# Expert weights in buffers of 2 MB, gate and up stored together, in a two-layer diffusion block

## The chip, the cores and the metric

The kernel runs on one core of a Trainium2 chip. The time is that of one execution on the device, in microseconds (us), from launch to the last result; lower is better. A core has TensorE (PE in the profile, with its weight loads as PEld), VectorE (DVE), ScalarE (ACT), GpSimd (POOL) and SyncE (SP), which here issues nearly all transfers. Sixteen DMA engines move data between DRAM and SBUF, the on-chip memory of 128 partitions.

## The reference, cut to what matters

A block of two layers works on 512 latent and 256 context tokens of width 1024. Each layer is a mixer (attention with retention in the first layer, RWKV with window attention in the second) and then 16 expert feed-forwards; an expert takes the 64 latent tokens that fit it best, in the first layer also 32 context tokens.

```python
def expert_choice_ffn(h, w_router, w_gate, w_up, w_down):
    cap = EC_FACTOR * N // N_EXPERTS                       # 64 latent, 32 context
    aff = softmax(h @ w_router)
    gate, idx = top_k(swapaxes(aff, 1, 2), cap)
    xs = h[idx]
    u = silu(xs @ w_gate) * (xs @ w_up)                    # per expert, 1024 x 1536 each
    y = (u @ w_down) * gate                                # per expert, 1536 x 1024
    return zeros.at[idx].add(y)

for layer in range(2):
    x_lat, x_ctx = mixers of the layer
    x_lat += g2 * expert_choice_ffn(h_lat, w[layer])
    if layer == 0:
        x_ctx += cg2 * expert_choice_ffn(h_ctx, w[layer])
return rmsnorm(x_lat, final_g)
```

All is float32. The three matrices of one expert hold 18.9 MB, those of the 16 experts of a layer 302 MB.

## The kernel before

`build` runs `mixer0`, `moe(0)`, `mixer1` and `moe(1)`. The change is in the two expert stages, `moe`.

An expert's 1536 hidden columns are worked in three chunks c of 512. `weights(c)` (L1909) takes four buffers from `wslot` (L1828) and loads the chunk: for i = 0 the gate rows k = 0 to 3 and the up rows k = 0 to 3, for i = 1 those of k = 4 to 7. A buffer is 128 partitions by 2048 float32: 1 MB, 8 KB in each partition, and `lay_out` (L2127) stores the weights in DRAM so that a partition's 8 KB are one contiguous row. `hidden` (L1919) multiplies the 64 latent tokens with gate and up, at each k first gate, then up (L1924, tile `gu`); `hidden_ctx` (L1933) does the same for 32 context tokens (L1937, tile `guc`). In the first layer the order of chunks is gu 0, guc 0, guc 1, gu 1, gu 2, guc 2. `turn` transposes the result. Then `down` (L1987) works three chunks of the down matrix, each in two buffers of 1 MB, for latent (L1992, `ydn`) and context tokens (L1996, `ydc`); in the last expert of the first layer all context chunks come first. The last down chunk of the kernel is loaded as four pieces of 512 KB.

The buffers are rings, used in turn. In the first layer the ring has 7 buffers (`open_ring(7)`, L730), in the second 12 (L1634) and 4 more of the pool `ring2` (L1824). A load into a buffer waits until TensorE has read what the buffer held. All these loads are issued in order by SP (L1915 and L2024). TensorE's order is written out by hand (`manual_schedule`), that of the other engines is the planner's.

`after` (L1822, L1873, L1960) names pairs of buffers that must not load too early. Into each buffer of such a pair POOL copies a few values of a late result (L1834), so that its load waits for that result: the logits of the router, the first selected tokens, the first context selection. In the second layer these are the pairs 6 and 7, the first four down buffers.

At the end of the second layer `fin` (L2063) takes three buffers of the ring again: the final gain in the first, four output tiles in the other two. When the first layer's stage closes, `mixer1` places its own tiles where the ring was, among them `lv` (loaded at L846).

Of the kernel before, what the change touches and what calls it, by code (L numbers as in the profile page):

```python
# [11 lines left out]
F32 = mybir.dt.float32  # L12
# [8 lines left out]
D = 1024  # L21
# [3 lines left out]
E, FF = 16, 1536  # L25
# [74 lines left out]
class Kern:  # L100
# [203 lines left out]
    def mixer0(self):  # L304
        nc, io, tc = self.nc, self.io, self.tc
# [41 lines left out]
        for t in range(6):  # L347
# [6 lines left out]
            for k0 in range(0, 8, 4):  # L354
# [4 lines left out]
                for i in range(4):  # L359
                    dst, src = aT[k0 + i][:, 128 * t:128 * t + 128], pt[:, 128 * i:128 * i + 128]  # L360
# [11 lines left out]
        for k in range(8):  # L372
            for (a, b, v) in ((0, 256, 1), (256, 768, 0)):
                x = aT[k][:, a:b]
# [352 lines left out]
        self.in_st = ExitStack()  # L727
        self.inp = self.in_st.enter_context(tc.tile_pool(name="in1", bufs=2))
        tc.swap_default_side()
        self.open_ring(7)  # L730

    def out_weights(self, l, w):

# [57 lines left out]
    def mixer1(self):  # L791
        nc, io, tc = self.nc, self.io, self.tc
# [771 lines left out]
        while min(nj.values()) < 6 or fins or min(nfin) < 2 or win:  # L1564
# [7 lines left out]
            for sl in slots:  # L1572
                if sl.gen is None and sets:
                    ok = [k for k in units if np_[k] < min(6, nj[k] + 2)
                          and all((tile_of[k[0]][np_[k]], 2 * k[1] + i) in fed for i in range(2))]
                    if ok:
                        k = min(ok, key=lambda k: np_[k])
# [32 lines left out]
            if wo is not None and min(nj.values()) < 6:  # L1610
                if not proj:
                    ready = [t for t in (3, 4, 2, 5) if nfin[t - 2] == 2 and lack[t]] + [
                        t for t in (3, 4, 2, 5) if 4 in lack[t]]
                    if ready:
                        t = ready[0]
# [15 lines left out]
            self.x[t] = self.xp.tile([128, D], F32, name=f"x{t}")  # L1631
            nc.sync.dma_start(self.x[t], xd[t - 2])
        tc.swap_default_side()
        self.open_ring(12)  # L1634
        st_f.close()
        self.route_open(1)
        routes = []
# [53 lines left out]
    def moe(self, l, out=None):  # L1691
        nc, io, tc = self.nc, self.io, self.tc
# [4 lines left out]
        ctx_on = l == 0  # L1697
# [102 lines left out]
        def split(g, pieces=1):  # L1800

            g.yh = mw.tile([128, D], F32R, name="yh", bufs=1)
            g.yl = mw.tile([128, D], F32R, name="yl", bufs=1)
            n = D // pieces
            for i in range(pieces):
                s = slice(n * i, n * i + n)
                nc.scalar.activation(g.yh[:, s], g.y[:, s], AF.Copy, scale=g.gate[:, 0:1])
                nc.vector.scalar_tensor_tensor(g.yl[:, s], g.y[:, s], g.gate[:, 0:1], g.yh[:, s].bitcast(F32),
                                               OP.mult, OP.subtract)

        def scatter(g):
            for t in range(g.n):
                for h in range(2):
                    pb = self.bank("scp")
                    s, w = slice(512 * h, 512 * h + 512), g.back[:, 128 * t:128 * t + 128]
                    nc.tensor.matmul(pb, w, g.yh[:, s], start=True, stop=False)
                    nc.tensor.matmul(pb, w, g.yl[:, s], start=False, stop=True)  # L1817
                    xs = self.x[g.a + t][:, s]
                    nc.vector.tensor_tensor(xs, pb, xs, OP.add)  # L1819
                yield None  # L1820

        taken, after = [0], {1: self.lgt[0:64, 1, 0:1]} if ctx_on else {}  # L1822

        more = 0 if ctx_on else 4  # L1824
        if more:
            wp = st.enter_context(tc.tile_pool(name="ring2", bufs=more))

        def wslot(nm):  # L1828
            pool = wp if taken[0] % (self.slots + more) >= self.slots else self.ring
            t = pool.tile([128, 2048], F32, name=nm, tag="ring")  # L1830

            w = after.get(taken[0] // 2)
            if w is not None:
                nc.gpsimd.tensor_copy(t[0:64, 0:1], w)  # L1834
            taken[0] += 1
            return t
# [5 lines left out]
        def at(e, place, gen, result=None):  # L1842
            shade.setdefault((e, place), []).append((gen, result))

        def run(e, place):
            for gen, result in shade.pop((e, place), ()):
                r = next(gen, None)
                if result is not None:
                    result[0][result[1]] = r
# [28 lines left out]
        for e in range(E):  # L1878
# [17 lines left out]
            def turn(c, sg, sc):  # L1896
                pt = self.bank("utp")
                for b in range(4):
                    nc.tensor.transpose(pt[:, 64 * b:64 * b + 64], sg[:, 128 * b:128 * b + 128], self.ident[0:64, 0:64])  # L1899
                nc.scalar.activation(uT[:, 4 * c:4 * c + 4], pt[:, 0:256].rearrange("p (b s) -> p b s", b=4), AF.Copy)  # L1900
                if ctx_on:
                    pt = self.bank("utc")
                    for b in range(2):
                        nc.tensor.transpose(pt[:, 64 * b:64 * b + 64], sc[:, 128 * b:128 * b + 128],  # L1904
                                            self.ident[0:64, 0:64])
                    nc.vector.tensor_copy(uTc[:, 4 * c:4 * c + 4].rearrange("p (h b) s -> p b h s", h=2),  # L1906
                                          pt[:, 0:128].rearrange("p (b h s) -> p b h s", b=2, h=2))

            def weights(c):  # L1909

                ws = [], []
                for i in range(2):
                    for w, wt in zip(("moe_w_gate", "moe_w_up"), ws):
                        t = wslot("we")
                        nc.sync.dma_start(t, io[w][l, e, c, i])  # L1915
                        wt += [t[:, 512 * k:512 * k + 512] for k in range(4)]
                return ws

            def hidden(ws):  # L1919
# [26 lines left out]
            if ctx_on and e == 0:  # L1946
# [4 lines left out]
                ws = weights(0)  # L1951
# [4 lines left out]
                ws = weights(1)  # L1956
# [7 lines left out]
            for c in range(3):  # L1964
# [5 lines left out]
                else:  # L1970
                    ws = weights(c)
# [15 lines left out]
            def down(c, wt, lat):  # L1987
                for i in range(4):
                    f = 4 * c + i
                    if lat:  # L1990
                        for h in range(2):
                            nc.tensor.matmul(y[64 * h:64 * h + 64, :], uT[:, f], wt[i][:, 512 * h:512 * h + 512],  # L1992
                                             start=f == 0, stop=f == 11, tile_position=(0, 64 * h))
                    else:
                        for j in range(4):
                            nc.tensor.matmul(yc[32 * j:32 * j + 32, 0:256], uTc[:, f], wt[i][:, 256 * j:256 * j + 256],  # L1996
                                             start=f == 0, stop=f == 11, tile_position=(0, 32 * j))
# [18 lines left out]
                        return gen  # L2016
            wts = []
            for c in range(3):
                wt = []
                for i in range(2):  # L2020
                    t, src = [v.rearrange("p (f n) -> p f n", f=2) for v in (wslot("wd"), io["moe_w_down"][l, e, c, i])]

                    for n in ((0, 2),) if (l, e, c) != (1, E - 1, 2) else ((0, 1), (1, 2)):
                        nc.sync.dma_start(t[:, n[0]:n[1]], src[:, n[0]:n[1]])  # L2024
                    wt += [t[:, 0], t[:, 1]]
                wts.append(wt)
                if ctx_on and e + 1 == E:

                    if c == 0:
                        turn(*prev)  # L2030
                    down(c, wt, False)
                    continue
                for lat in ((False, True), (True, False))[c % 2] if ctx_on else (True,):
                    down(c, wt, lat)
                if c == 0:
                    turn(*prev)
                run(e, 3 + c)
# [11 lines left out]
            if a == 1:  # L2049
                def late(g=g, e=e):  # L2050
                    split(g, 1 if e + 1 < E else 2)
                    if e + 1 < E:
                        yield
                    yield from scatter(g)
                gen = late()
                if e + 1 < E:
                    for p in (0, 1, 2, 3, 3):
                        at(e + 1, p, gen)
                elif out is None:
                    self.tail = gen  # L2060
                else:

                    fin, norms = [self.ring.tile([128, 2048], F32, name="fin", tag="ring") for _ in range(3)], []  # L2063
                    nc.gpsimd.dma_start(fin[0][:, 0:D], io["final_g"].rearrange("(o n) -> o n", o=1).to_broadcast([128, D]))
                    for t, _ in enumerate(gen):
                        for n in norms:
                            next(n, None)
                        norms.append(self.final(out, t, fin))
                        next(norms[-1])
                    for n in norms:  # L2070
                        drain(n)
# [10 lines left out]
    def final(self, out, t, buf):  # L2082

        nc = self.nc
        x, o, fg = self.x[2 + t], buf[1 + t // 2][:, D * (t % 2):D * (t % 2) + D], buf[0][:, 0:D]
        rs = self.norm_tile(x, o, apply=False)
        yield
        nc.vector.scalar_tensor_tensor(o, x, rs, fg, OP.mult, OP.mult)
        nc.sync.dma_start(out[0, 128 * t:128 * t + 128], o)
# [36 lines left out]

def lay_out(arrays):  # L2127

    for n in ("moe_w_gate", "moe_w_up"):
        w = arrays[n].reshape(2, E, 2, 4, 128, 3, 512)  # L2130
        arrays[n] = np.ascontiguousarray(w.transpose(0, 1, 5, 2, 4, 3, 6)).reshape(2, E, 3, 2, 128, 2048)
    w = arrays["moe_w_down"].reshape(2, E, 3, 2, 2, 128, D)
    arrays["moe_w_down"] = np.ascontiguousarray(w.transpose(0, 1, 2, 3, 5, 4, 6)).reshape(2, E, 3, 2, 128, 2048)


# [17 lines left out]
```

## Time and profile before

| | us |
|---|---|
| median of 3 runs | 3020.55 |
| lowest, highest of them | 3016.89, 3022.68 |
| the profiled execution | 3012.17 |
| its span, first to last instruction | 3010.4 |
| expert stage of layer 0, steady experts | 640 to 1420 |
| expert stage of layer 1, after its first expert | 2323 to 2990 |

The profiled execution lies 8.4 us below the median. "Issue" in the profile is time in which an engine waited for nothing that the profile shows. A wait is put down to what came last before the engine went on. Matmuls are pipelined, so a busy PE is not a PE at its peak, and a stretch in which PE waits a little before every matmul can look nearly full.

### The profile page before, as it was taken

The numbers are of one execution on the slowest core, as the hardware profiler recorded it, in microseconds if no ns is written. First come the engines' busy times: TensorE is split into PE (matmuls) and PEld (weight loads), VectorE is DVE, ScalarE is ACT, GpSimd is POOL, SyncE is SP. The second block draws the span as 40 slices with busy tenths as digits, with TensorE's granted clock in tenths as the row PEclk, the third lists the DMA queues.
The fourth block names the chain that finished last, engine by engine and source line by source line (L and its number), as shares of the span: only waits on it lengthen the run. The fifth ranks groups of instructions, "written<-read, shape, count | busy, mean of one in ns | idle before, by whom it ended". The sixth has DMA issues, their size and how long they took to land.

```text
span 3010.4 us, 48424 instructions
## 1 busy us (share of the span) xinstructions
PE 2708.7 (90%) x19606; PEld 1547.0 (51%) x19606; DVE 1324.3 (44%) x3546; ACT 741.4 (25%) x1718; POOL 472.4 (16%) x597
## 2 busy tenths in 40 slices
PE   7999999799999999999878888799987988888987
PEld 4787776544444444444466666587653332333322
DVE  4323664534234234322375777677654332223312
ACT  3212443211111111100263544266321111000111
POOL 2332002200000000000174553411210000000000
PEclk9999999799999999999987988899888999999999
DMA  9764001488988988888642334311349999999997
GB/s 328 249 242 163 26 12 64 156 355 337 362 343 339 362 333 349 361 332 362 245 124 80 92 95 125 107 36 31 117 181 375 420 420 420 420 420 420 420 420 319
DMA packets 217919, 779.52 MB, mean 259 GB/s; under 512 B 28919, under 2 KB 115360, under 8 KB 138080
## 3 DMA queue, kind: packets, MB, share of 16 engines
q1 hardware_dynamic: 210528, 752.33, 64.4%
q0 software_dynamic: 3872, 12.52, 1.2%
q10 hardware_dynamic: 3296, 11.58, 1.0%
q8 instruction: 155, 2.54, 0.3%
q14 instruction: 68, 0.56, 0.1%
HBM read 745.68 MB, written 30.67 MB: 258 GB/s over the span
## 4 chain that ended last, share of the span: by engine, by line
PE 57%; DMA 26%; DVE 9%; ACT 3%; POOL 2%; issue 2%; SPq 0%; POOLq 0%; ACTq 0%; DVEq 0%
DMA we<-in_moe_w_up_dram 18%; PE gu L1924 12%; DMA wd<-in_moe_w_down_dram 7%; PE ydn L1992 6%; PE guc L1937 4%; PE pj L926 3%; PE ydc L1996 3%; PE pj L411 2%; PE op L774 2%; PE pj L412 2%; PE pj L413 2%; PE op L1556 2%; PE adap L231 1%; PE sc L593 1%; PE pe L1398 1%
## 5 line engine op out<-in xcount | busy, mean ns | idle before, releaser
L1924 PE MATMUL gu<-we,xs 128*64 128x512 f32 x3072 | 721.3, 599 | 79.0 <-DMA we<-in_moe_w_up_dram 75.1
L1924 PEld LDWEIGHTS gu<-we,xs 128*64 128x64 f32 x3072 | 226.8, 137 | 537.7 <-issue 392.5
L1992 PE MATMUL ydn<-wd,uT 128*64 128x512 f32 x1536 | 352.9, 600 | 3.0 <-DMA wd<-in_moe_w_down_dram 2.1
L1930 DVE TENSOR_TENSOR sg<-gu,sg 64x512 f32<-64x512 f32 x96 | 66.5, 693 | 482.1 <-ACT sg L1929 481.5
L1929 ACT ACTIVATE sg<-gu 64x512 f32<-64x512 f32 x96 | 56.7, 591 | 872.1 <-PE gu L1924 872.1
L1776 POOL DMA_INDIRECT xg<-xnd,idx x22 | 20.9, 949 | 1276.0 <-DVE gate L1781 913.6
L1992 PEld LDWEIGHTS ydn<-wd,uT 128*64 128x64 f32 x1536 | 101.4, 137 | 200.6 <-issue 178.9
L1937 PE MATMUL guc<-we,xs 128*32 128x256 f32 x3072 | 183.7, 384 | 19.1 <-DMA we<-in_moe_w_up_dram 19.1
L926 PE MATMUL pj<-aL,wblk 128*128 128x512 f32 x504 | 159.8, 452 | 0.0
L1937 PEld LDWEIGHTS guc<-we,xs 128*32 128x32 f32 x3072 | 98.6, 111 | 96.6 <-DMA we<-in_moe_w_up_dram 26.3
L411 PE MATMUL pj<-ah,wblk 128*128 128x384 f32 (+1 forms) x320 | 109.5, 343 | 1.1 <-ACT ah L380 1.0
L926 PEld LDWEIGHTS pj<-aL,wblk 128*128 128x128 f32 x504 | 100.0, 212 | 18.6
L412 PE MATMUL pj<-al,wblk 128*128 128x384 f32 (+1 forms) x320 | 107.7, 337 | 0.3 <-DVE al L382 0.3
L413 PE MATMUL pj<-ah,wblk 128*128 128x384 f32 (+1 forms) x320 | 107.4, 336 | 0.0
L1819 DVE TENSOR_TENSOR x<-scp,x 128x512 f32<-128x512 f32 x144 | 92.4, 684 | 30.9 <-PE scp L1817 29.8
L1996 PE MATMUL ydc<-wd,uTc 128*32 128x256 f32 x1536 | 91.6, 383 | 2.1 <-DMA wd<-in_moe_w_down_dram 2.1
L1906 DVE COPY uTc<-utc 128x128 f32<-128x128 f32 x48 | 14.0, 292 | 177.1 <-PE utc L1904 176.7
L2047 DVE TENSOR_TENSOR yp<-ydn,gbc 64x512 f32<-64x512 f32 x64 | 44.1, 689 | 103.0 <-PE ydn L1992 100.0
L1796 DVE TENSOR_SCALAR xs<-xst,gm,modT 128x128 f32<-128x128 f32 (+1 forms) x88 | 34.9, 398 | 102.8 <-PE xst L1788 99.6
L1942 DVE TENSOR_TENSOR sc<-guc,sc 64x256 f32<-64x256 f32 x48 | 20.4, 425 | 126.7 <-ACT sc L1941 126.6
L1900 ACT ACTIVATE uT<-utp 128x256 f32<-128x256 f32 x96 | 36.0, 375 | 150.6 <-PE utp L1899 149.7
L1382 DVE STREAM_TRANSPOSE Zbd<-X 64x256 f16<-64x256 f16 x144 | 62.8, 436 | 23.4 <-ACT X L1376 21.0
(421 smaller groups left out, 4667.9 us busy)
## 6 DMA issues: line engine op xcount, KB each, us to landing
we<-in_moe_w_gate_dram SPq DMA_DIRECT2D x192, 1024.0 KB, 19.8
we<-in_moe_w_up_dram SPq DMA_DIRECT2D x192, 1024.0 KB, 9.9
wd<-in_moe_w_down_dram SPq DMA_DIRECT2D x190, 1024.0 KB, 10.7
adaw<-in_ada_w_dram SPq DMA_DIRECT2D x48, 1024.0 KB, 6.6
wraw<-in_od_w_in_dram SPq DMA_DIRECT2D x33, 512.0 KB, 4.3
wraw<-in_ev_w_in_dram SPq DMA_DIRECT2D x19, 512.0 KB, 6.9
fb<-B SPq DMA_DIRECT2D x24, 256.0 KB, 2.4
BK<-fb SPq DMA_DIRECT2D x24, 256.0 KB, 3.1
```

Of the source, the lines that this page charges most:

```text
L411: nc.tensor.matmul(pb[:m, :384], w[:, 0, k, 0:m], ah[k][:, t], start=k == 0, stop=False)
L412: nc.tensor.matmul(pb[:m, :384], w[:, 0, k, 0:m], al[k][:, t], start=False, stop=False)
L413: nc.tensor.matmul(pb[:m, :384], w[:, 1, k, 0:m], ah[k][:, t], start=False, stop=k == 7)
L774: nc.tensor.matmul(o, a[:, i, k], cut[h, k][:, j], start=k + i + j == 0, stop=k == 7 and i == 1)
L926: nc.tensor.matmul(pb[:, :n], w[:, i, k], a[j][:, k], start=k + i + j == 0, stop=k == 7 and i == 1)
L1382: nc.vector.transpose(Zd[h], X[hd[h]])
L1819: nc.vector.tensor_tensor(xs, pb, xs, OP.add)
L1924: nc.tensor.matmul(gu[64 * j:64 * j + 64, :], g.xs[:, k, 64 * a:64 * a + 64], ws[j][k], start=k == 0, stop=k == 7, tile_position=(0, 64 * j))
L1930: nc.vector.tensor_tensor(sg, gu[64:128], sg, OP.mult)
L1937: nc.tensor.matmul(guc[32 * j:32 * j + 32, 0:256], q.xs[:, k, 32 * a4:32 * a4 + 32], ws[j // 2][k][:, 256 * (j % 2):256 * (j % 2) + 256], ...
L1992: nc.tensor.matmul(y[64 * h:64 * h + 64, :], uT[:, f], wt[i][:, 512 * h:512 * h + 512], start=f == 0, stop=f == 11, tile_position=(0, 64 * h))
L1996: nc.tensor.matmul(yc[32 * j:32 * j + 32, 0:256], uTc[:, f], wt[i][:, 256 * j:256 * j + 256], start=f == 0, stop=f == 11, tile_position=(0 ...
```

## The change

Gate and up of a chunk half are stored as one tensor `moe_w_gate_up`, so that a partition's row holds the four gate rows and behind them the four up rows: 16 KB contiguous in DRAM, 2 MB in one load. A down chunk becomes one load of 2 MB with rows of 16 KB too. An expert's 18 loads become 9. The first layer's ring has 4 buffers of 2 MB (64 KB in each partition, 56 KB before), the second layer's 6 and 2 more (128 KB in all, as before). The keys of `after` count buffers and not pairs, and so name the same bytes. The last down chunk is still loaded in four pieces of 512 KB. `fin` takes two buffers of 2 MB.

```diff
@@ end of mixer0 @@
-        self.open_ring(7)
+        self.open_ring(4)
@@ end of mixer1 @@
-        self.open_ring(12)
+        self.open_ring(6)
@@ moe @@
-        more = 0 if ctx_on else 4
+        more = 0 if ctx_on else 2
...
-            t = pool.tile([128, 2048], F32, name=nm, tag="ring")
+            t = pool.tile([128, 4096], F32, name=nm, tag="ring")
-            w = after.get(taken[0] // 2)
+            w = after.get(taken[0])
...
                 for i in range(2):
-                    for w, wt in zip(("moe_w_gate", "moe_w_up"), ws):
-                        t = wslot("we")
-                        nc.sync.dma_start(t, io[w][l, e, c, i])
-                        wt += [t[:, 512 * k:512 * k + 512] for k in range(4)]
+                    t = wslot("we")
+                    nc.sync.dma_start(t, io["moe_w_gate_up"][l, e, c, i])
+                    for j in range(2):
+                        ws[j].extend(t[:, 2048 * j + 512 * k:2048 * j + 512 * k + 512] for k in range(4))
...
-                for i in range(2):
-                    t, src = [v.rearrange("p (f n) -> p f n", f=2) for v in (wslot("wd"), io["moe_w_down"][l, e, c, i])]
-                    for n in ((0, 2),) if (l, e, c) != (1, E - 1, 2) else ((0, 1), (1, 2)):
-                        nc.sync.dma_start(t[:, n[0]:n[1]], src[:, n[0]:n[1]])
-                    wt += [t[:, 0], t[:, 1]]
+                t, src = [v.rearrange("p (f n) -> p f n", f=4) for v in (wslot("wd"), io["moe_w_down"][l, e, c])]
+                step = 4 if (l, e, c) != (1, E - 1, 2) else 1
+                for n in range(0, 4, step):
+                    nc.sync.dma_start(t[:, n:n + step], src[:, n:n + step])
+                wt = [t[:, f] for f in range(4)]
...
-                    fin, norms = [self.ring.tile([128, 2048], F32, name="fin", tag="ring") for _ in range(3)], []
+                    fin, norms = [self.ring.tile([128, 4096], F32, name="fin", tag="ring") for _ in range(2)], []
@@ final @@
-        x, o, fg = self.x[2 + t], buf[1 + t // 2][:, D * (t % 2):D * (t % 2) + D], buf[0][:, 0:D]
+        x, o, fg = self.x[2 + t], buf[1][:, D * t:D * t + D], buf[0][:, 0:D]
@@ lay_out @@
-    for n in ("moe_w_gate", "moe_w_up"):
-        w = arrays[n].reshape(2, E, 2, 4, 128, 3, 512)
-        arrays[n] = np.ascontiguousarray(w.transpose(0, 1, 5, 2, 4, 3, 6)).reshape(2, E, 3, 2, 128, 2048)
-    w = arrays["moe_w_down"].reshape(2, E, 3, 2, 2, 128, D)
-    arrays["moe_w_down"] = np.ascontiguousarray(w.transpose(0, 1, 2, 3, 5, 4, 6)).reshape(2, E, 3, 2, 128, 2048)
+    w = np.stack([arrays.pop(n).reshape(2, E, 2, 4, 128, 3, 512) for n in ("moe_w_gate", "moe_w_up")])
+    arrays["moe_w_gate_up"] = np.ascontiguousarray(w.transpose(1, 2, 6, 3, 5, 0, 4, 7)).reshape(2, E, 3, 2, 128, 4096)
+    w = arrays["moe_w_down"].reshape(2, E, 3, 4, 128, D)
+    arrays["moe_w_down"] = np.ascontiguousarray(w.transpose(0, 1, 2, 4, 3, 5)).reshape(2, E, 3, 128, 4096)
```

## Rows read from the trace of the kernel before

**Rows 1.** The page's span in 40 equal slices: DMA busy tenths and rate.
```profile
DMA  9764001488988988888642334311349999999997
GB/s 328 249 242 163 26 12 64 156 355 337 362 343 339 362 333 349 361 332 362 245 124 80 92 95 125 107 36 31 117 181 375 420 420 420 420 420 420 420 420 319
```

**Rows 2.** Windows: stretch and length, busy us of each engine, granted clock, DMA share, GB/s.
```profile
640.00:1420.00 780.00, 761.96 (x6670) 335.01 (x6672) 266.53 (x811) 95.89 (x200) 8.43 (x9) 1.00 0.87 349
...
2283.00:2323.00 40.00, 35.87 (x179) 14.04 (x180) 19.87 (x88) 7.22 (x14) 1.33 (x5) 0.90 1.00 393
2323.00:2990.00 667.00, 587.39 (x2624) 209.51 (x2622) 173.77 (x488) 69.41 (x141) 7.16 (x8) 1.00 1.01 418
```

**Rows 3.** The page's costliest groups: L1937, its idle time before and the releaser.
```profile
L1937 PE MATMUL guc<-we,xs 128*32 128x256 f32 x3072 | 183.7, 384 | 19.1 <-DMA we<-in_moe_w_up_dram 19.1
```

**Rows 4.** Waits of PE from 640 to 1420: us in total, times, longest.
```profile
PE guc L1937 <- DMA we<-in_moe_w_up_dram: 18.0, 14, 2.6
```

**Rows 5.** Chain of work, one expert of layer 0: start, us, what.
```profile
760.20 6.87 PE gu L1924 x32
767.07 1.89 PE guc L1937 x32
768.96 4.79 DMA we<-in_moe_w_up_dram
...
773.79 1.92 PE guc L1937 x28
...
776.22 13.88 PE gu L1924 x64
...
790.62 3.59 PE guc L1937 x64
```

**Rows 6.** Timeline of another expert: context result of chunk 0 and its transpose.
```profile
715.43 0.42 DVE L1942 TENSOR_TENSOR sc<-guc,sc 64x256 f32<-64x256 f32 x1
...
718.73 0.28 PE L1904 MATMUL utc<-ks,sc 64*128 64x64 f32 x2
```

**Rows 7.** Waits of PE at the stage's first expert (575 to 640).
```profile
PE gu L1924 <- DMA we<-in_moe_w_up_dram: 2.2, 1, 2.2
```

**Rows 8.** Waits of PE at the stage's last expert (1420 to 1485).
```profile
PE ydc L1996 <- DMA wd<-in_moe_w_down_dram: 2.1, 2, 1.3
```

**Rows 9.** Timeline of SP in layer 1: start, us to issue, what.
```profile
2337.84 0.33 SPq L1915 DMA_DIRECT2D we<-in_moe_w_gate_dram  x1
2340.33 0.33 SPq L1915 DMA_DIRECT2D we<-in_moe_w_up_dram  x1
2342.81 0.33 SPq L1915 DMA_DIRECT2D we<-in_moe_w_gate_dram  x1
```

**Rows 10.** DMA queues from 2340 to 2640: packets, MB, share (q0: gathers, 4 KB).
```profile
q1 hardware_dynamic: 17054, 124.17, 99.8%
q0 software_dynamic: 432, 1.57, 1.3%
```

**Rows 11.** The same, 500 to 560; q10 stores xn in 4 KB rows.
```profile
q10 hardware_dynamic: 576, 2.10, 8.7%
```

**Rows 12.** DMA rate in 40 slices from 2127 to 2160 (`wo`, 2 KB rows).
```profile
GB/s 0 27 226 417 405 405 417 387 400 410 412 407 412 412 422 429 332 219 138 292 228 46 30 0 0 0 0 0 0 0 0 0 0 0 0 0 10 372 258 25
```

**Rows 13.** Timeline of SP at the start of layer 1's stage.
```profile
2247.97 0.33 SPq L1915 DMA_DIRECT2D we<-in_moe_w_up_dram  x1
2260.43 0.33 SPq L255 DMA_DIRECT2D brow<-in_ada_b_dram  x1
...
2283.07 10.70 SPq L2024 DMA_DIRECT2D wd<-in_moe_w_down_dram  x6
```

**Rows 14.** Chain of work at the start of layer 0's stage: the first gather.
```profile
575.57 4.09 DMA xg<-xnd,idx
```

**Rows 15.** Waits of SP from 1446 to 1500.
```profile
SPq L846 <- PE ydn L1992: 15.3, 1, 15.3
...
SPq L878 <- DVE yp L2047: 0.7, 1, 0.7
```

More of the change, by code (lines that the diff above doesn't have):

```diff
@@ L2018, in moe @@
             for c in range(3):
-                wt = []
-                for i in range(2):
-                    t, src = [v.rearrange("p (f n) -> p f n", f=2) for v in (wslot("wd"), io["moe_w_down"][l, e, c, i])]
-                    for n in ((0, 2),) if (l, e, c) != (1, E - 1, 2) else ((0, 1), (1, 2)):
-                        nc.sync.dma_start(t[:, n[0]:n[1]], src[:, n[0]:n[1]])
-                    wt += [t[:, 0], t[:, 1]]
+                t, src = [v.rearrange("p (f n) -> p f n", f=4) for v in (wslot("wd"), io["moe_w_down"][l, e, c])]
[3 more added lines that the diff above has]
+                wt = [t[:, f] for f in range(4)]
                 wts.append(wt)
```

## The prediction

> **What bounds the kernel now.** I read the span in slices first [rows 1]. The two expert stages differ. From slice 9 to slice 19 (layer 0) the transfers run at 332 to 362 GB/s; from slice 32 to slice 39 (layer 1) they stand at 420 GB/s without a dip. The windows by stage say what that means [rows 2]: in layer 0's steady experts PE is busy for 761.96 of 780 us at full granted clock and DMA for 87%, so PE sets the pace; in layer 1 the DMA engines are full (1.01) and PE's 587 of 667 us are stretched by small waits for weights. So one layer needs fewer gaps on PE and the other a higher transfer rate. The change touches both.
>
> In layer 0 the list of groups and the waits name the one gap that is left [rows 3, 4]: PE waits for an up load ahead of guc, 19.1 us in all, 18.0 of them in 14 experts of the steady stretch, 1.3 us each. The chain of one expert shows where [rows 5]: gu 0 and guc 0 run, half of guc 0 ends at 768.96, and at that moment the up load of chunk 1's second half is issued; PE goes on at 773.79. Seven buffers explain it. Chunk 0 holds four; three are left for chunk 1, which needs four. The seventh buffer's successor has to wait until guc 0 has passed its half.
>
> In layer 1 SP issues 1 MB every 2.49 us [rows 9], which is the rate of the DMA engines; depth of buffers does not matter there, only how long a row takes.
>
> **The change part by part.**
>
> *Layer 0, four buffers of 2 MB.* In the old ring half of a pair waits for the pair four back and half for the pair three back. In the new one all of it waits for the pair four back, which is released earlier. I follow one expert in its own times. A lone load of 1 MB took 4.8 us from issue to use (768.96 to 773.79) [rows 5]; one more MB takes 2.49 [rows 9], so 2 MB alone take 7.3 us, and 5.0 behind another load.
> - Chunk 1, second half: issued when the previous expert's last down chunk is done, 760.20; landed 767.5. Without the wait PE needs it at 760.20 + 6.87 + 3.59 + 1.8 = 772.5. Margin 5.0 us.
> - Chunk 2, first half: issued at the half of guc 0, 768.96; landed 776.3; needed after gu 1, at 774.8 + 6.9 = 781.7. Margin 5.4 us.
> - Chunk 2, second half: issued at the end of guc 0, 770.7; lands behind the load before it, 781.3; needed 3.5 us into gu 2, 785.2. Margin 3.9 us, the smallest.
> - The down chunks are issued at the halves and ends of gu 1 and at the half of guc 2 and are needed 6 to 8 us after they land by the same count.
>
> So nothing waits, and the 19.1 us go. What is late next is PE itself, apart from one thing: the transpose behind guc 1 reads DVE's product of chunk 0, done at 715.85 where PE now comes at 718.73 [rows 6]; 1.3 us earlier it still comes 1.6 us after it. That gap covers the step; without it up to 1.3 us an expert would come back.
>
> *Layer 0, both ends.* In the first expert gu 1 waits 2.2 us for the same buffer [rows 7]; the new ring has it loaded: 2.2 us gained. In the last expert the third down chunk's two loads wait for guc 2's half and for its end, and PE waits 2.1 us [rows 8]. In the new ring the whole chunk is issued at the half, and takes 7.3 us; PE needs it 1.8 + 0.5 + 3.7 = 6.0 to 6.4 us after that half. 0.9 us stay: 1.2 gained. Sum for layer 0: 19.1 + 2.2 + 1.2 = 22.5 us.
>
> *Behind layer 0.* `lv` waits 15.3 us for the last down buffer, since it lies where that buffer was [rows 15]; in a ring of four its place belongs to chunk 2's second half, free 20 us earlier. That is worth nothing: the third load behind it waits for DVE's yp at 1485.4 in any case, and the weights of the projection stand behind that.
>
> *Layer 1, rows of 16 KB.* The trace has no weight row of 16 KB; I bound its time from both sides. Durations: 4 KB rows, stored, took 8.7% of 16 engines for 60 us, 83.5 us for 512 rows, 163.1 ns each [rows 11], and gathered ones about the same (1.3% for 384 rows, 162.5 ns) [rows 10]; 8 KB rows took 99.8% of 16 engines for 300 us, 4790 us for 124.17 MB or 15157 rows, 316.1 ns each [rows 10]. Both contain one small completion packet to eight rows (576 - 512 and 17054 - 15157). 4 KB more cost 153.0 ns, so 10.1 ns of a row are fixed, and a 16 KB row takes 622.1 ns for 632.2: 1.6% less. From 2283 to 2990 there are 276 loads of 1 MB, 138 of the new ones with 8 rows on each engine: 138 x 8 x 10.1 ns = 11.1 us. The other bound is the rate: 2 KB rows moved at 410 GB/s (mean of the 13 slices from 417 to 429) [rows 12], 79.9 ns each, 8 KB rows at 420, 312.1 ns; then only 2.5 ns are fixed, and the gain is 2.8 us. I take 11.1, because 4 and 8 KB rows are nearest in size and the 2 KB stretch is 11 us long; 2.8 stays as the bound.
>
> [...]
>
> *Start of layer 1.* Six loads are issued ahead of `brow`, six behind it, and the down loads at 2283.07 behind POOL's copy [rows 13]; six loads and 1 MB for `brow` and its like take 7 x 2.49 = 17 us from 2261 on, so they land shortly before that. The keys of `after` leave that point where it is. If the planner puts three or four of the new loads ahead of `brow`, nothing changes; if only two, 2 MB come later: up to 5.0 us lost.
>
> *What costs.* The first gather of tokens takes 4.09 us [rows 14] and runs beside the next weight loads. It has 64 rows, four on an engine; if each lets one weight row pass, rows twice as long add 4 x 0.31 = 1.2 us at most, and nothing if it is ahead of them. I take 0.6 in layer 0. In layer 1 the same is hidden: 4 MB of down weights are then in flight. Half as many issues on SP (0.33 us each) and copies on POOL save nothing, as both engines are idle there; the last four 512 KB pieces and `fin` keep their places.
>
> **Sum.** 22.5 + 11.1 - 0.6 = 33.0 us. Against the profiled execution: 3012.2 - 33.0 = 2979.2. The median of the runs is 8.4 us above that execution, and I carry this over: 2987.5, rounded 2988.
>
> **The rivals.**
> - *The rate stays.* Either long rows are cut into packets of 8 KB, or bytes alone count. For it: the rates by row size. Against it: the durations. Layer 1 gives 0 to 2.8 us: 2988 + 8.3 to 11.1, about 2997.
> - *The wait moves.* A buffer is now usable only when 2 MB have landed, and released only as a whole. If 2 MB take 4 us longer than I count, chunk 2 waits instead of chunk 1, and the 19.1 us come back: 3007. Against it are the margins of 3.9 us and more, and 13% of idle DMA time.
> - *Slower: long rows move slower.* Place: layer 1, where every us of transfer counts. 22 us gained in layer 0 are lost when the 667 us stretch by 3.3%, at 404 GB/s. The slowest sustained rate of these loads is 393 GB/s, from 2283 to 2323, with gathers beside them [rows 2]; at that rate 667 x (418/393 - 1) = 42 us are lost: 2988 + 11 + 42 = 3041. Against it: from 4 KB to 8 KB rows time grew by less than the bytes. [...]
>
> **How the numbers follow.** My forecast, 2988 with its own bounds, has 0.56; the unchanged rate 0.22; the wait that moves 0.10; slower rows 0.06; 0.06 is left for what I do not see. Low end: the forecast without the carried 8.4 us and with 2 us for the gather and the first expert, 2977. High end: the unchanged rate, 2997, with 5 us for the start of layer 1 and 3 us of scatter of the runs, 3005. Some 0.2 lie outside. About 0.2% (6 us) is what a measurement of this kernel can tell from no change. Faster by more than that is below 3014.5: forecast, unchanged rate and moved wait, 0.88; the rest is split, 0.06 and 0.06.
>
> **What would show it.** In the profile after: no wait of guc for a `we` load in layer 0, PE busy for over 99% from 640 to the stage's end, an expert every 54.4 us instead of 55.7 (780 / 14); packets of 16 KB, half as many; in layer 1 a steady 425 to 427 GB/s, SP's issues 4.9 us apart, and a stage shorter by 11 us. Wrong if guc's wait is still there or gu or ydn has a new one, if packets are still 8 KB, if the rate in layer 1 is 420 or below, or if the stages between the two expert stages change by more than 5 us.

## The result, and the profile after

| | before, us | after, us |
|---|---|---|
| median (lowest to highest), 4 runs each on one chip | 3019.18 (3016.89 to 3022.68) | 2971.35 (2967.24 to 2975.60) |
| the profiled execution | 3012.17 | 2972.21 |
| its span | 3010.4 | 2970.4 |

The ratio is 0.9853, with a 95% interval from 0.9833 to 0.9872: 47.8 us faster between the medians, 40.0 us between the two profiled executions. The prediction was 2988, from 2977 to 3005. The direction and the two mechanisms came out; the time lies below the range.

The span in slices after the change, against [rows 1] (DMA busy tenths, then rate):

```profile
DMA  9765001488988988988642233310349999999997
GB/s 329 244 246 175 27 12 57 172 333 353 371 356 355 371 345 367 365 355 355 216 126 73 86 108 120 111 32 28 118 184 377 426 427 427 427 426 427 426 427 314
```

In layer 1 the floor is 426 to 427 GB/s where it was 420. The windows by stage, against [rows 2] (columns as there):

```profile
640.00:1400.00 760.00, 760.00 (x6738) 335.65 (x6732) 269.41 (x817) 96.01 (x200) 8.44 (x9) 1.00 0.90 361
...
2293.00:2950.00 657.00, 559.28 (x2634) 208.09 (x2632) 173.79 (x488) 69.54 (x141) 7.16 (x8) 1.00 1.00 424
```

The second window ends about where the loads do, as in [rows 2]: 424 GB/s against 418. PE is busy for all of 760 us in layer 0. The groups of the page say the same of guc, against [rows 3]; the row behind it shows what PE still waits for at `ydc`, against [rows 8]:

```profile
L1937 PE MATMUL guc<-we,xs 128*32 128x256 f32 x3072 | 172.6, 380 | 0.0
...
L1996 PE MATMUL ydc<-wd,uTc 128*32 128x256 f32 x1536 | 90.6, 380 | 1.4 <-DMA wd<-in_moe_w_down_dram 1.4
```

The busy time of guc fell too, from 183.7 us to 172.6, for the same 3072 matmuls. That is the first sign of where the surplus lies. One expert in the chain of work, against [rows 5] (start, us, what):

```profile
699.61 5.58 PE gu L1924 x26
705.19 0.58 PE rkp L1726 x4
705.77 7.04 PE guc L1937 x128
...
714.89 13.88 PE gu L1924 x64
...
731.22 3.59 PE guc L1937 x64
```

guc 0 and guc 1, 128 matmuls together, now run in one piece. I cut both profiled executions at the same events to see where the 40.0 us went:

| stretch (from ... to) | before | after | change | predicted |
|---|---|---|---|---|
| start to the first gu of expert 0 | 582.64 | 587.69 | +5.1 | +0.6 |
| expert 0, to the first gu of expert 1 | 64.77 | 58.86 | -5.9 | -2.2 |
| 14 experts, to the first gu of the last | 778.75 | 750.53 | -28.2 | -18.0 |
| last expert, to the first `pj` (L926) of the mixer | 68.84 | 65.31 | -3.5 | -2.3 |
| mixer, to the loads of x (L1632) | 737.10 | 739.34 | +2.2 | 0 |
| to the first down load of layer 1 | 50.97 | 51.00 | 0.0 | 0 |
| layer 1, from that load to the end | 727.33 | 717.70 | -9.6 | -11.1 |

(The 2.3 of the last expert are the 1.2 of the prediction and the 1.1 of guc's 19.1 that belong there.) Three questions come out of the table: why the steady experts gave 28.2 us where 18.0 were recorded as waits, whether it is the row that makes layer 1 faster, and what costs 5 us at the start.

### The profile page after: what moved, and what is told of

It reads as the page before. It is cut to its first block, busy times and chain, and to the rows that moved or that the text cites. A ratio compares the mean times of both kernels' runs of the same rounds, so it can differ in the third digit from the quotient of the medians.

```text
span 2970.4 us, 47837 instructions
## 1 busy us (share of the span) xinstructions
PE 2660.2 (90%) x19606; PEld 1535.4 (52%) x19606; DVE 1322.9 (45%) x3546; ACT 742.6 (25%) x1718; POOL 471.4 (16%) x591
## 4 chain that ended last, share of the span: by engine, by line
PE 64%; DMA 19%; DVE 9%; POOL 3%; ACT 3%; issue 2%; SPq 0%; POOLq 0%; ACTq 0%; DVEq 0%
PE gu L1924 13%; PE ydn L1992 9%; DMA wd<-in_moe_w_down_dram 8%; DMA we<-in_moe_w_gate_up_dram 8%; PE guc L1937 6%; PE ydc L1996 3%; PE pj L926 3%; PE pj L411 2%; PE pj L412 2%; PE pj L413 2%; PE op L774 2%; PE op L1556 2%; PE adap L231 2%; PE sc L593 1%; PE scp L1816 1%
## 5 line engine op out<-in xcount | busy, mean ns | idle before, releaser
L1924 PE MATMUL gu<-we,xs 128*64 128x512 f32 x3072 | 687.9, 597 | 83.5 <-DMA we<-in_moe_w_gate_up_dram 83.4
L1924 PEld LDWEIGHTS gu<-we,xs 128*64 128x64 f32 x3072 | 216.7, 137 | 520.5 <-issue 408.5
L1992 PEld LDWEIGHTS ydn<-wd,uT 128*64 128x64 f32 x1536 | 107.9, 137 | 205.3 <-issue 187.0
L1937 PE MATMUL guc<-we,xs 128*32 128x256 f32 x3072 | 172.6, 380 | 0.0
L926 PE MATMUL pj<-aL,wblk 128*128 128x512 f32 x504 | 158.1, 448 | 0.0
L1937 PEld LDWEIGHTS guc<-we,xs 128*32 128x32 f32 x3072 | 96.4, 110 | 68.4 <-issue 7.5
L926 PEld LDWEIGHTS pj<-aL,wblk 128*128 128x128 f32 x504 | 99.0, 210 | 18.4
L1906 DVE COPY uTc<-utc 128x128 f32<-128x128 f32 x48 | 14.0, 291 | 172.6 <-PE utc L1904 172.1
L1996 PEld LDWEIGHTS ydc<-wd,uTc 128*32 128x32 f32 x1536 | 47.6, 110 | 43.9 <-issue 15.2
```

What stands on the lines that cost most here:

```text
L926: nc.tensor.matmul(pb[:, :n], w[:, i, k], a[j][:, k], start=k + i + j == 0, stop=k == 7 and i == 1)
L1924: nc.tensor.matmul(gu[64 * j:64 * j + 64, :], g.xs[:, k, 64 * a:64 * a + 64], ws[j][k], start=k == 0, stop=k == 7, tile_position=(0, 64 * j))
L1937: nc.tensor.matmul(guc[32 * j:32 * j + 32, 0:256], q.xs[:, k, 32 * a4:32 * a4 + 32], ws[j // 2][k][:, 256 * (j % 2):256 * (j % 2) + 256], ...
```

## Experiments

### Depth alone: ring8, and the other way, ring6

ring8 is the kernel before, with one more buffer of 1 MB in the first layer: 8 MB as in the change, with the old loads and rows.

```diff
-        self.open_ring(7)
+        self.open_ring(8)
```

> The kernel before with eight buffers of 1 MB in the first layer and nothing else: rows of 8 KB, 18 loads an expert, as before. Theory (depth alone makes layer 0 faster): no wait of guc for an up load, the 14 steady experts take about 750 us (778.8 before, 750.5 in the changed kernel), layer 1 stays at 420 GB/s and as long as before; the whole is 28 to 38 us faster than before. Rival (one load of 2 MB instead of two of 1 MB makes it): the wait of guc is still there, the 14 experts take 770 us or more, the whole is within 10 us of before.

Measured: 2979.86 us (2979.30 to 2982.43), ratio 0.9879 (0.9863 to 0.9895). The 14 steady experts took 750.85 us, as after the change; layer 1 took 727.25, as before. In the stretch from 640 to 1420 one wait of guc for a load is left:

```profile
PEld guc L1937 <- DMA we<-in_moe_w_up_dram: 0.2, 1, 0.2
```

So the depth alone gives the whole gain of the steady experts, and it is 27.9 us here. That the buffers are 2 MB and usable only as a whole costs nothing, against the rival of the wait that moves.

ring6 takes a buffer away instead, to see what a recorded wait is worth when there are more of them.

```diff
-        self.open_ring(7)
+        self.open_ring(6)
```

> The kernel before with six buffers of 1 MB in the first layer. It measures what a wait of TensorE costs beside what the profile records as idle. With seven buffers the 14 steady experts lost 28 us to a ring of eight, of which 18 are recorded as waits in 14 pieces. Theory (each wait costs some 0.6 us more than its record, for draining and refilling the array): lost time is the recorded waits plus 0.5 to 0.8 us for each. Rival (a share of the wait, 1.6 times the record): lost time is 1.6 times the recorded waits, however many pieces. In both more waits than with seven; the 14 experts take over 800 us.

Measured: 3114.44 us (3109.92 to 3118.97), ratio 1.0314 (1.0289 to 1.0340). The 14 experts took 865.87 us (658.26 to 1524.13), 115.3 more than unhindered. The waits of PE and of its weight loads in that stretch (us in total, times, longest):

```profile
PEld guc L1937 <- DMA we<-in_moe_w_up_dram: 36.4, 14, 3.7
PEld guc L1937 <- DMA we<-in_moe_w_gate_dram: 32.7, 14, 4.2
PE guc L1937 <- DMA we<-in_moe_w_up_dram: 29.7, 14, 3.2
PEld gu L1924 <- DMA we<-in_moe_w_up_dram: 26.0, 26, 2.2
PE guc L1937 <- DMA we<-in_moe_w_gate_dram: 25.9, 14, 3.7
PEld guc L1937 <- issue: 19.7, 75, 0.8
PE gu L1924 <- DMA we<-in_moe_w_up_dram: 9.1, 9, 1.3
```

PE's rows add up to 64.7 us in 37 pieces, those of the weight loads to 95.1, and 115.3 were lost. The theory gives 83 to 94 us (64.7 and 0.5 to 0.8 for each of the 37), the rival 104; both fall short, the rival by less. The draining and refilling of the array, by which the theory explained its part, was a guess of mine; no view shows it. The same in the kernel before (647 to 1426), which the prediction read only in its PE row:

```profile
PEld guc L1937 <- DMA we<-in_moe_w_up_dram: 24.8, 14, 3.1
PE guc L1937 <- DMA we<-in_moe_w_up_dram: 18.0, 14, 2.6
PEld guc L1937 <- issue: 6.5, 18, 0.8
PEld gu L1924 <- DMA we<-in_moe_w_up_dram: 1.2, 2, 0.8
```

PE 18.0, PEld 26.0, lost 28.2. Both times the record of the matmuls holds 56 to 64% of what a stall takes, and that of the weight loads 82 to 92%. One stall of the kernel before shows where the rest is; first the matmuls, then the weight loads:

```profile
767.00 5.81 PE L1937 MATMUL guc<-we,xs 128*32 128x256 f32 x100
773.79 1.92 PE L1937 MATMUL guc<-we,xs 128*32 128x256 f32 x28 [0.99 <-DMA we<-in_moe_w_up_dram]
```

```profile
767.00 5.32 PEld L1937 LDWEIGHTS guc<-we,xs 128*32 128x32 f32 x100 [0.81 <-issue]
773.79 1.44 PEld L1937 LDWEIGHTS guc<-we,xs 128*32 128x32 f32 x28 [1.47 <-DMA we<-in_moe_w_up_dram]
```

The two parts last 8.71 us from 767.00 to 775.71. The same 128 matmuls (guc 0 and guc 1) took 7.04 us in the expert shown above: 1.7 us are lost. 0.99 is recorded as waiting; the two busy pieces, 5.81 and 1.92, are together 0.7 us longer than 7.04. So part of the stall is booked as busy time; on which of the matmuls, no run shows. The weight loads record 1.47. In ring6 the issue row of guc is 13.2 us above that of the kernel before and the granted clock 0.97 instead of 1.00 in the stretch; how the 20 us that its weight loads do not record divide between the two, no run tells apart.

### The row in layer 1: cols1, rows8 and cols4

All three are the changed kernel with the loads of layer 1 alone altered. cols1 cuts each load into two of 1 MB, by columns, so that a row is 8 KB:

```diff
-                    nc.sync.dma_start(t, io["moe_w_gate_up"][l, e, c, i])
+                    src = io["moe_w_gate_up"][l, e, c, i]
+                    for h in range(2 if l else 1):
+                        w = slice(2048 * h, 2048 * h + 2048) if l else slice(0, 4096)
+                        nc.sync.dma_start(t[:, w], src[:, w])
...
-                step = 4 if (l, e, c) != (1, E - 1, 2) else 1
+                step = (4 if l == 0 else 2) if (l, e, c) != (1, E - 1, 2) else 1
```

> The changed kernel, but in layer 1 each buffer of 2 MB is filled by two loads of half the columns: rows of 8 KB, loads of 1 MB as before the change, same buffers. Theory (the length of a row sets the rate): layer 1 runs at 420 GB/s again and takes about 10 us longer than in the changed kernel; layer 0 unchanged; 2981. Rival (bytes alone, or the depth of the ring, set it): 426 GB/s, 2971.

Measured: 2981.78 us (2975.53 to 2983.82), ratio 0.9879 (0.9863 to 0.9896). Layer 1 took 727.3 us from its first down load. The whole gain of layer 1 is gone.

rows8 keeps the loads at 2 MB and stores the weights of layer 1 so that a partition gets two rows of 8 KB from different places (the down matrix in the same way, not shown):

```diff
+                    if l:
+                        nc.sync.dma_start(t.rearrange("p (h n) -> p h n", h=2), io["moe_w_gate_up1"][e, c, i].rearrange("h p n -> p h n"))
+                    else:
+                        nc.sync.dma_start(t, io["moe_w_gate_up"][l, e, c, i])
...
+    g = arrays["moe_w_gate_up"][1].reshape(E, 3, 2, 128, 2, 2048)
+    arrays["moe_w_gate_up1"] = np.ascontiguousarray(g.transpose(0, 1, 2, 4, 3, 5))
```

> The changed kernel, but layer 1's weights are stored so that a load of 2 MB takes two rows of 8 KB for each partition: 2 MB loads with rows of 8 KB, same buffers. Theory (the length of a row sets the rate): 420 to 421 GB/s, about 9 us longer than the changed kernel, 2981. Rival (fewer and larger loads set it, the completion and the gap between loads being what costs): 426 GB/s, 2972.

Measured: 2981.50 us (2970.92 to 2984.17), ratio 0.9877 (0.9861 to 0.9894). Layer 1 took 727.9 us. Loads of 2 MB with short rows gain nothing, so the gain belongs to the row and not to the load or to the number of issues.

cols4 goes the other way, four loads of 512 KB with rows of 4 KB (the same edit as cols1, in steps of 1024 columns):

> The changed kernel with the loads of layer 1 cut into four pieces of 512 KB, so that rows are 4 KB there; layer 0 as in the changed kernel. A third point on row length, after 8 KB (layer 1 in 727.3 us from its first down load to the end) and 16 KB (717.7). By the difference of packet times seen so far (12 to 13 ns fixed in every row) 8 KB to 4 KB costs twice what 16 KB to 8 KB does: layer 1 takes about 19 us longer than 727.3, some 746, and a 4 KB row some 163 ns. If instead the gain belongs to the load of 2 MB with its 16 KB rows alone (a shorter queue, fewer issues), rows of 4 KB give a layer 1 within 5 us of 727.3. Should SP's issues, four times as many, set the pace, the issue rows stand closer than 0.4 us and the DMA share falls below 0.97.

Measured: 3000.45 us (2994.51 to 3003.45), ratio 0.9931 (0.9915 to 0.9947). Layer 1 took 747.1 us (2252.31 to 2999.4), 1.1 from the 746 expected. That 746 came from doubling the step of 9.6 us; the 12 to 13 ns beside it, over 2208 rows, would have given 26 to 29 us and some 755, which was not measured. The weight queue in the 500 us from 2400 to 2900 (packets, MB, share of 16 engines), in cols4, in cols1 and after the change:

```profile
DMA packets 56103, 204.51 MB, mean 409 GB/s; under 512 B 6234, under 2 KB 6234, under 8 KB 56080
...
q1 hardware_dynamic: 55360, 201.57, 101.1%
```

```profile
DMA packets 29175, 209.97 MB, mean 420 GB/s; under 512 B 3241, under 2 KB 3241, under 8 KB 3881
...
q1 hardware_dynamic: 28433, 207.04, 99.8%
```

```profile
DMA packets 15193, 213.38 MB, mean 427 GB/s; under 512 B 1687, under 2 KB 1687, under 8 KB 2327
...
q1 hardware_dynamic: 14452, 210.46, 99.1%
```

The engines are full in all three and move 409, 420 and 427 GB/s. Layer 1 takes 747.1, 727.3 and 717.7 us: halving the number of rows gives 19.8 us and then 9.6, half as much for half as many rows. On the prediction's count of 1104 rows of 16 KB on each engine, 9.6 us are 8.7 ns for each row saved, and 19.8 us over 2208 rows are 9.0 ns: one price for both steps. The packet times of the three views (164, 316 and 617 ns for 4, 8 and 16 KB, from share and count) would make it 13 to 15 ns; their shares, 101.1 to 99.1%, differ between the kernels, so I go by the time of the stage.

### Long rows in smaller loads: parts1

The changed kernel, with each load of layer 1 cut by partitions into two of 64 partitions, 1 MB each, rows of 16 KB (the down loads in the same way, not shown).

```diff
+                    src = io["moe_w_gate_up"][l, e, c, i]
+                    for h in range(2 if l else 1):
+                        w = slice(64 * h, 64 * h + 64) if l else slice(0, 128)
+                        nc.sync.dma_start(t[w], src[w])
```

> The changed kernel, but in layer 1 each buffer of 2 MB is filled by two loads of half the partitions: rows of 16 KB, loads of 1 MB. Theory (the length of a row): 425 to 427 GB/s, only the completion packets double, 9 ns on each engine for 2 MB, 1.2 us in all; 2972. Rival (the number of loads sets the rate): 420 GB/s and 10 us longer, 2981, as with two loads of half the columns.

Measured: 3604.31 us (3516.10 to 3653.83); the lowest of them is 545 us above the median after the change. Both expectations, 2972 and 2981, were wrong. (The 9 ns in the first are in the trace: the 4-byte packets of the kernel before have a median of 9 ns.) The run does not tell load size from row length, since something larger came in. The same 500 us of it, in the longest of the four runs:

```profile
DMA packets 8527, 107.69 MB, mean 215 GB/s; under 512 B 1665, under 2 KB 1665, under 8 KB 2049
...
q1 hardware_dynamic: 8084, 105.96, 99.5%
```

The engines are as full as before and move half: a row of 16 KB takes 99.5% of 16 x 500 us over 6467 rows, 1231 ns, against 617 ns by the same count after the change. What makes a row of these loads take twice as long, no run here shows. rows8 and cols1 settled in parts1's place what it was meant to settle.

### The start of layer 0: skip0 and ring31

The first weight load of layer 0 is issued at 567.04 after the change and at 556.76 before, and the first gather takes 8.80 us instead of 4.09 [rows 14]. The chain after, and SP's waits from 530 to 580 in it:

```profile
575.91 8.80 DMA xg<-xnd,idx
584.71 0.04 issue
584.75 1.11 PE xst L1788 x8
```

```profile
SPq L1914 <- DMA xnd<-xn: 31.2, 2, 19.8
SPq L1914 <- POOL we L1834: 9.5, 2, 8.5
SPq L1914 <- PE lg L1688: 3.9, 1, 3.9
```

The loads now wait for the router (`xnd`, `lg`), and then run together with the gather. Before, SP waited for `SPq L1915 <- POOL x L779` here. Two kernels ask which buffer it is. skip0 passes over the first buffer, so that the second is loaded first:

```diff
+        if ctx_on:
+            self.ring.tile([128, 4096], F32, name="skip", tag="ring")
```

> The changed kernel with one buffer passed over at the start of the first layer, so that the first load goes into the second buffer and the buffer that the first one had is used by the fourth load. Theory (the first buffer of 16 KB lies where the router's tiles were, its load is therefore 10 us late, and the first gather meets it): the first load is issued near 557 instead of 567, the gather takes about 4 us instead of 8.8, the first gu starts about 5 us earlier; 2966. Rival (rows of 16 KB beside the gather make it long): the gather stays near 8 us, and the time at 2971.

Measured: 2971.70 us (2962.31 to 2972.25), ratio 0.9839 (0.9820 to 0.9857). The first load came at 567.61, the gather took 8.77 us, so the theory was wrong. The order of the buffers does not matter.

ring31 opens three of the four buffers where the ring was, below the 56 KB of the old ring, and the fourth later, with the stage's own pool:

```diff
-        self.open_ring(4)
+        self.open_ring(3)
...
-        more = 0 if ctx_on else 2
+        more = 1 if ctx_on else 2
```

> The changed kernel with the first layer's four buffers of 2 MB cut in two pools: three in the ring (48 KB in each partition, below the 56 KB of the old ring) and the fourth opened in the expert stage, as the second layer does it. Theory (a ring of 64 KB reaches into the place of the router's tiles, so all its loads wait for them): the first load is issued near 557 instead of 567, the first gather takes 4 to 5 us instead of 8.8, the first gu starts 4 to 5 us earlier, the steady experts stay at 51 to 57 us; 2966. Rival (rows of 16 KB lengthen the gather): first load early, gather still over 7 us, 2971.

Measured: 2977.19 us (2967.51 to 2977.73), ratio 0.9850 (0.9828 to 0.9872). The first load came at 557.82 and the gather took 4.07 us, with SP's wait as in the kernel before:

```profile
SPq L1914 <- POOL x L779: 25.8, 1, 25.8
```

So it is the ring of 64 KB as a whole, opened at that point, that makes the first load late, not the length of the rows. Which tile of the router the last 8 KB meet was not tried. The rows have a small share: in ring8, with 64 KB and the old rows, the load comes as late (567.69), and the gather takes 7.55 us, 1.25 less than in the first profile of the change and 1.7 less than in the second (9.23).

The first gu comes at 583.67 in ring31, 4.0 us earlier than after the change, yet ring31 was not faster: 2977.19 against the 2966 expected. In its profile the mixer between the stages takes 5.2 us longer than after the change (744.5 against 739.3), and the first expert 62.1 us against 58.9. The windows from 600 to 610 (columns as in [rows 2]) and guc 0 in the timeline, ring31 first:

```profile
600.00:610.00 10.00, 9.43 (x84) 4.91 (x86) 7.26 (x32) 2.02 (x5) 1.09 (x2) 0.66 0.34 103
```

```profile
602.55 5.79 PE L1937 MATMUL guc<-we,xs 128*32 128x256 f32 x64
```

```profile
600.00:610.00 10.00, 7.25 (x92) 4.27 (x92) 9.21 (x43) 2.74 (x6) 1.08 (x2) 1.00 0.32 83
```

```profile
605.18 3.66 PE L1937 MATMUL guc<-we,xs 128*32 128x256 f32 x64
```

In ring31 TensorE's granted clock falls to half a second time in the first expert (0.51 from 600 to 605); after the change it stays at 1.00 and the same 64 matmuls take 3.66 us instead of 5.79. This second fall is in the profiles of before (clock 0.75 in that window), before2 (0.66), ring6 (0.50 from 600 to 605), ring8 (0.68), skip0 (0.69) and ring31 (0.66), and not in after, after2, cols1, rows8 and cols4 (1.00 in all five), whose first layer is that of the change. That looks like the code, but the first layer of parts1 is the same too, and its profile has the fall (guc stands in L1940 there):

```profile
600.00:610.00 10.00, 7.25 (x55) 4.03 (x55) 8.35 (x37) 2.36 (x5) 0.91 (x1) 0.73 0.21 71
```

```profile
607.01 5.80 PE L1940 MATMUL guc<-we,xs 128*32 128x256 f32 x64
```

Its first expert took 62.1 us, like ring31's. So the code alone does not decide it: the same first layer went either way, and the 3.3 us between 58.86 and 62.12 go with the fall. What the rows show ahead of it is how early the clock rose the first time. The first 32 matmuls of gu, which begin at half clock (after the change at 587.69, with 0.56 from 585 to 590 and 1.00 from 590 to 595), took 7.73 to 7.94 us in the five profiles without a second fall and 8.00 to 8.52 in the seven with it. The two groups are only 0.06 us apart and were sorted after the fact; what decides it stays open.

### The same kernels again: before2 and after2

The prediction carried 8.4 us from the profiled execution of before to the median. A second profile of either kernel shows what varies from one execution to the next.

> The kernel before once more, profiled on the same chip as the others. If the first profile's 3012.2 us was short by chance against the median of 3017 to 3019, some stage is longer here: the mixers by the clock (theory, up to 4 us each), not the steady experts of layer 0 (778.8) nor the rate in layer 1 (420 GB/s).

Measured: 3016.76 us for the run with the profile, span 3014.9. The steady experts took 782.67 us (778.75 in the first profile), with a wait of 18.8 us on guc in PE's row; layer 1 took 727.2. The theory was wrong in where it looked: the steady experts were 3.9 us longer, and the mixer between the stages 1.7 us shorter.

> The changed kernel once more, for a second profile. Theory: where its times are set by the code, they return: first weight load of layer 0 issued within 2 us of 567, the first gather about 8.8 us, 14 steady experts in 750.5, layer 1 in 717.7. The 3.3 us of the first expert (a second stretch at half clock, absent in the first profile) and the 8 us of the mixer are then expected to vary, if they are chance; if they belong to the code, the first expert takes 58.9 us again and the granted clock stays at 1.00 from 600 to 610.

Measured: 2972.29 us (2971.15 and 2973.44), ratio 0.9851 (0.9773 to 0.9929). First load at 568.12, gather 9.23 us, expert 0 in 58.6, 14 experts in 750.53, layer 1 in 717.8, clock 1.00 from 600 to 610. These durations came back within 0.5 us, the first load 1.1 us later; in the kernel before, whose ring waits, the 14 experts came back within 4. Cut at the same events, the second pair differs by 43.3 us: 32.1 in the 14 experts (28.2 in the first pair), 9.4 in layer 1, 6.6 in the first expert. That the clock stayed at 1.00 again does not show that the code decides it, since in parts1 it did not.

The mixer between the stages, which is the same code in all, took from 728.9 us (rows8, granted clock of the whole span 0.957) to 744.5 (ring31, 0.948) in the twelve profiles. These 15.6 us are as wide as the scatter of whole times of one kernel (3008.35 to 3023.51 for the kernel before, beside ring31 and rows8), and two profiles of the change lie 0.1 apart; the 2.2 us between before and after are well inside it.

## Why the prediction was right or wrong, point by point

- **The wait of guc: mechanism right, term mis-sized.** The fourth 2 MB take the wait away, nothing else waits in its place, and PE is busy throughout, as predicted; the wait did not move. The step that failed is "18.0 of them in 14 experts of the steady stretch, 1.3 us each": it took the price from PE's row of waits. It was 28.2 us, 2.0 each, and 32.1 between the second pair of profiles (and an expert takes 53.6 us, not 54.4). The rows of the weight loads held 26.0. Even [rows 5] had it: guc 0 and guc 1 last from 767.07 to 775.71 there, 8.64 us, and guc 2 of the same expert, 3.59 us for 64 matmuls, says 7.2 for the 128.
- **First expert: 2.2 predicted, 5.9 measured.** With the clock's second fall, in ring8, skip0, ring31 and parts1, expert 0 took 61.5 to 62.2 us, 2.5 to 3.3 less than before; that is the wait for chunk 1, and 2.2 was nearly right. The other 3 us are a fall of the clock that this execution did not have. In parts1 the same first layer has it, so these 3 us are luck as far as the runs show, and the prediction said nothing of them.
- **Last expert: 2.3 predicted, 3.5 measured.** `ydc` still waits, 1.4 us (0.9 predicted), so 0.7 of the 3.5 come from there. The other 2.8, against 1.1 predicted for guc, fit an under-priced wait of guc as in the 14 experts; no run separates them.
- **Start of layer 0: 0.6 predicted, 5.1 measured.** The bound of 1.2 us for rows twice as long was nearly good (1.25 and 1.7 us between ring8 and the two profiles of the change). The step that failed is that the loads would stand where they stood: the prediction took no account of 8 KB more in the ring being claimed while the router's tiles live there. This is the transfer that comes 10 us later and then collides with the gather.
- **Layer 1: 11.1 predicted, 9.6 measured.** The fixed cost of a row is there, 8.7 to 9.0 ns by the time of the stage against the 10.1 of the prediction; the lower bound of 2.5 ns, from rates of rows of 2 KB, was far off, and so was the rival of the unchanged rate. Slower long rows did not come: 426 to 427 GB/s.
- **Start of layer 1: 0 predicted, 0.0 measured.** Three loads ahead of `brow` and three behind it, the case for which no loss was predicted:

```profile
2203.52 1.96 SPq L1914 DMA_DIRECT2D we<-in_moe_w_gate_up_dram  x3
2230.57 0.33 SPq L255 DMA_DIRECT2D brow<-in_ada_b_dram  x1
...
2231.89 1.73 SPq L1914 DMA_DIRECT2D we<-in_moe_w_gate_up_dram  x3
2252.73 10.99 SPq L2023 DMA_DIRECT2D wd<-in_moe_w_down_dram  x3
```

- **`lv`: cost right, reason wrong.** It still waits as long for `ydn`, against [rows 15], so its place did not come free 20 us earlier; the third load behind it still waits for `yp`, which is why nothing came of it either way:

```profile
SPq L846 <- PE ydn L1992: 15.3, 1, 15.3
...
SPq L878 <- DVE yp L2046: 0.7, 1, 0.7
```

- **From profile to median.** The sum gave 2979.2 for a profiled execution; it was 2972.2, 7.0 us less (10.2 for guc, 3.7 and 1.2 for the first and last expert, and back 4.5, 2.2 and 1.5 for the start, the mixer and layer 1, each rounded). The 8.4 us carried on top are best read as scatter of one execution: the profiled run after lies 0.9 us above its median, not below, and the second profile of before came out 4.6 us longer than the first. The low end of 2977 had left these 8.4 out already, so they do not explain a time below it. What does is the 10.2 of guc: had it given only the 18.0 of the prediction, the median would have been some 2982, inside the range.

## What to carry to other kernels

Where matmuls stall, price a stall by the length of the stretch against an unhindered one of the same instructions, or by the waits of the weight loads; PE's own row of waits held some 60% of it here. Where the DMA engines are full, count rows and not loads: each row cost about 9 ns beside its bytes here, the same from 4 to 8 KB as from 8 to 16 KB, and cutting the loads by partitions cost half the rate (215 GB/s against 427), far more than the row length gave. When a buffer grows, look at what lives in its new bytes at the moment that it is opened: here 8 KB made the first load 10 us late. Before a small gain is put down to the code, look for it in every run with the same code: here some 3 us of the first expert came back in parts1, whose first layer is that of the change.

## What was not expected of the hardware

Loads into 64 neighbouring partitions ran at half the rate (215 GB/s against 427), though the loads of both halves were in flight one behind the other (39.1 us from issue to landing, where 1 MB at this rate takes 4.9) and the engines showed 99.5% busy. And a second fall of the granted clock to half in the first expert (6.8 us long in the first profile of before) came in seven profiles and stayed away in five, with the same first layer on both sides, and was worth 3 us, not far from the 4.0 us by which ring31 started earlier.
